# One output product for the last FFN of a four-FFN trunk: all its middle values at once, transposed by DMA, with P7 ahead of P3

## Chip, cores and metric

The kernel runs on one core of one Trainium2 chip. The metric is the device time of one execution in microseconds (us). All inputs lie in HBM at the start, and the output has to lie there at the end. A profiled execution also gives a span, from the first to the last instruction of the program, and a record of every instruction and DMA.

## What is computed

The reference is a trunk of two layers over 512 positions of width 1024, in float32. Each layer is a half-weighted SwiGLU FFN, a token mixer, and a second FFN; a final RMSNorm follows.

```python
def swiglu(x, w_in, w_out):
    g, u = jnp.split(x @ w_in, 2, axis=-1)       # w_in 1024 x 5632, w_out 2816 x 1024
    return (jax.nn.silu(g) * u) @ w_out

for i in range(DEPTH):                            # DEPTH = 2
    h = h + 0.5 * swiglu(rms_norm(h, ffn1_norm[i]), ffn1_w_in[i], ffn1_w_out[i])
    hn = rms_norm(h, mix_norm[i])
    m = recurrent_mixer(hn, ...) if i == 0 else spatial_gating_mixer(hn, ...)
    h = h + m
    h = h + 0.5 * swiglu(rms_norm(h, ffn2_norm[i]), ffn2_w_in[i], ffn2_w_out[i])
return rms_norm(h, final_norm)
```

So there are four FFNs, and the change is about the last of them and the final norm.

## The kernel before

**Number format.** Every float32 operand of a large product is split into a high part (`hi`, float32r, by ScalarE, line 99) and the rest (`lo`, by VectorE, line 90). A product is then three matmuls: hi x hi, lo x hi, hi x lo (lines 416 to 418). In the profile `whi`, `wlo` are the parts of a weight block, `hi`, `lo` those of a left operand.

**Seven products.** A product is cut into quarters and done with seven block products instead of eight (Strassen's method in Winograd's form): P1, P2, P5, P6, P3, P7, Q4 (function `seven`). Each has a left factor (A11, A12, S1, S2, S4, S3, A22, table `LEFT`) and a weight block; S1 = A21 - A22, S2 = S1 - A11, S4 = A12 + S2, S3 = -S2 - A22. Sums of weight blocks are made by loading one block and adding another, with an accumulating DMA of GpSimd (POOL, line 141) or on VectorE (`raw<-raw,raw`). The results gather in PSUM banks A (P1, then P6 and P7 on top), B (P2), C (P5, then P3 on top) and Q (Q4; in an output product with the final norm Q4 uses A). After a product, VectorE adds the bank to the hidden state `x`, which stays in SBUF.

**Sub-steps.** All work of TensorE is one list, `subs`: one entry is one product over one cut of the inner dimension, with 12 matmuls of 512 columns (6 where the cut has one block). At each entry the main loop at the end of the file emits, in this order, what is hooked as "pre", the splits of weight blocks up to three entries ahead (`SPLIT_AHEAD`), what is hooked as "mid" and "rest", new loads, the matmuls, and what is hooked as "end" and "late". Loads go out on SP in the order of the list, as long as fewer than ten blocks (`RAW_BUFS`) are held. Each engine works through its instructions in this order.

**An FFN.** The 22 blocks of 128 middle values are one pair (2 blocks, `pair_plain`, products named `p`) and five chunks of four (`chunk`, 14 sub-steps each). A chunk's result must be transposed before it can be the left operand of the output product (`out_blocks`). There are two ways. On TensorE, a 128x128 block at a time, through PSUM (`Group.turn`, line 270, tiles `e<-ident,c`) with a copy out by ScalarE. Or by the DMA crossbar (`Group.cross`): ScalarE sorts the halves of each float32 into two 16-bit planes (`pl`), SP issues a transposing DMA (`dt<-pl`), ScalarE merges the planes again five and six sub-steps later.

The first three FFNs collect all six groups of middle values and then do one output product over all of them (`FF_WHOLE`); all their transposes go by the crossbar, and the order of the 42 sub-steps is written out in `CHAIN`. The name `P62` is product P6 over cut 2; cut 0 is the pair and has half the work.

The fourth FFN is divided into three parts (`FF_PARTS`): pair and one chunk, two chunks, two chunks. Each part ends with its own output product of 14 sub-steps, in the order P1, P2, P6, P5, P7, Q4, P3 (`FinalNorm.ORDER`). In each part the first group goes by the crossbar, the second through TensorE.

**The end.** `FinalNorm` takes squares, roots and one Newton step as soon as rows of `x` are complete. P3 is the last product. Its first cut is held back (`held`), and in the last sub-step both cuts are multiplied for rows 0 and then for rows 1, with two matmuls by an identity (`gather`, line 1069) that add row block 1 of `x` into the bank. `last` then completes rows 0 and 1, and in between, for t = 0, it also scales and stores rows 2 and 3 (`both(2, 0)`, `scaled(3, 1)`, `both(3, 0)`).

Of the kernel before, what the change touches and what calls it, by code (L numbers as in the profile page):

```python
# [27 lines left out]

FF_PARTS = (("p", 4), (4, 4), (4, 4))
FF_WHOLE = (("p", 4, 4, 4, 4, 4),)

RAW_BUFS = 10
# [21 lines left out]
def trunk(ctx: ExitStack, tc: tile.TileContext, a: dict, out: bass.AP):  # L56
# [312 lines left out]
    def seven(block, cuts, left, w, posts, order=None, own=False, apart=False, joined=None, opening=None,  # L369
# [14 lines left out]
        def mm_of(prod, ci):  # L384
            name, fresh = banks[prod]
            pairs = cuts[ci]

            def mm(sub):
                if fresh and ci == 0:
                    for s in range(2):  # L390
                        bk[name, s] = bank(name)[:, :w]
                if prod == joined and ci == 0:
                    held.extend((sub, q, i) for q, i in enumerate(pairs))
                    return
                if opening and prod == "P1":
                    qs = list(enumerate(pairs))
                    for n, (q, i, m, s) in enumerate([(q, i, m, s) for q, i in qs for m in range(3) for s in range(2)]
                                                     if ci == 0 else
                                                     [(q, i, m, s) for m in range(3) for q, i in qs for s in range(2)]):
                        if n == (4 if ci else 6):  # L400
                            opening[ci]()
                        nc.tensor.matmul(bk[name, s], left(prod, i, s)[m == 1], (sub.lo if m == 2 else sub.hi)[:, q, :],
                                         start=(i, m) == (0, 0), stop=(i, m) == (cuts[-1][-1], 2))
                    for s in range(2 * ci):
                        posts[prod](s, bk[name, s])
                    return
                for s in range(2):
                    ps = bk[name, s]
                    k = {} if fresh else dict(skip_group_check=True)
                    if prod == joined and also is not None:  # L410
                        also(s, ps)
                    for sb, q, i in (held if prod == joined else []) + [(sub, q, i) for q, i in enumerate(pairs)]:
                        zh, zl = left(prod, i, s)
                        wh, wl = sb.hi[:, q, :], sb.lo[:, q, :]
                        end = i == cuts[-1][-1]
                        nc.tensor.matmul(ps, zh, wh, start=fresh and i == 0, stop=False, **k)  # L416
                        nc.tensor.matmul(ps, zl, wh, start=False, stop=False, **k)  # L417
                        nc.tensor.matmul(ps, zh, wl, start=False, stop=end, **k)  # L418
# [12 lines left out]
        for prod, ci in order:  # L431
# [3 lines left out]
            def new(k, n, plus=None, wait=2):  # L435
                b = lambda k, n: block(k, n, cuts[ci])
                return raw_of(b(k, n), [P, len(cuts[ci]), w], plus and b(*plus), wait)

            tile = then = tile_then = None
            if chain:  # L440
                if prod in ("P1", "P2"):
                    r = new(int(prod == "P2"), 0)
                elif prod == "P5":
                    r = raw[11, ci] = new(0, 0, (0, 1))
                elif prod == "P6":
                    r, tile, then = raw[11, ci], new(1, 1), block(1, 0, cuts[ci])
# [11 lines left out]
            elif prod == "P5":  # L458
# [10 lines left out]
            elif prod == "P6" and joined:  # L469

                tile, r, then = new(0, 1, (1, 1)), new(0, 0), block(1, 0, cuts[ci])
                raw[6, ci], raw[12, ci] = r, tile
            elif prod == "P6" and far(ci):
                r, then = raw[11, ci], block(1, 0, cuts[ci])
            elif prod == "P6":
                r, tile, then = raw[11, ci], new(1, 1), block(1, 0, cuts[ci])
                raw[22, ci] = tile
            elif prod == "P3":
                r = new(1, 1) if far(ci) or joined else raw[22, ci]
            elif prod == "P7":  # L480
                r = raw[12, ci] if joined or not own else new(0, 1, (1, 1), 2 + ci if far(ci) else 2)
            else:
                r = raw[6 if joined else 11, ci]
            subs.append(Sub(r, mm_of(prod, ci), None, tile, then, tile_then))
        return order

# [158 lines left out]
    def out_blocks(w, k0, groups, scale, norm=None, order=None, own=False, soon={}, swap=False, p2_lag=0, chain=False):  # L645
# [8 lines left out]
            bases[cut[0]] = r  # L654
            r += 2 * len(cut)

        gs, held, c5 = {}, [], []

        def block(k, c, cut):
            r0 = (bases[cut[0]] + k * len(cut)) * P  # L660
# [23 lines left out]
                take()  # L684

        def p5(s, ps):
            if ends:
                c5.append(ps)
            else:
                upd(2 + s, 1, ps, scale)  # L690

        def p6(s, ps):
            upd(s, 1, ps, -scale)
# [8 lines left out]
            final(s, 1, "A12", s)  # L702

        def p7(s, ps):
            if ends:
# [12 lines left out]

# [5 lines left out]
        def q4(s, ps):  # L724
            if held:
                second()
            upd(2 + s, 0, ps, scale)
            final(2 + s, 0, "A21", s)

        at0, ends = len(subs), hasattr(norm, "last")  # L730
        if ends:
            order = norm.ORDER
        order = seven(block, cuts, left_of(lambda: [gs[i] for i in range(len(n))]), 512,
                      dict(P1=p1, P2=p2, P5=p5, P6=p6, P3=p3, P7=p7, Q4=q4), order, own, not ends,
                      "P3" if ends else None, also=norm.gather if ends else None, chain=chain)

        sums_of = dict(P1=lambda ci: gs[ci].s2(), P2=lambda ci: gs[ci].s4(), P5=lambda ci: gs[ci].s3()) if chain else {}
# [195 lines left out]

    def ffn(w_in, w_out, norm):
        f0 = 0
        chain = not hasattr(norm, "last")
        all_parts = FF_WHOLE if chain else FF_PARTS
        for i, sizes in enumerate(all_parts):
            groups, p0, pair, first = [], f0, None, not subs
            for j, n in enumerate(sizes):  # L940
                if n == "p":
                    groups.append(Group(1))
                    groups[-1].whole = chain
                    pair = lambda g=groups[-1], f0=f0: pair_plain(w_in, f0, g, first)
                    if not first:
                        pair()
                    f0 += 2
                else:
                    groups.append(Group(n // 2))
                    groups[-1].whole = chain  # L950
# [3 lines left out]
            last, mixed = i == len(all_parts) - 1, "p" in sizes and not chain  # L954
            if mixed:
                groups.reverse()
            soon = {("Q4", len(groups) - 1): 3} if last and isinstance(norm, TileNorm) else {}
            gs = out_blocks(w_out, p0, [g.n for g in groups], 0.5, norm if last else None, CHAIN if chain else None,
                            own=True, soon=soon, swap=mixed, p2_lag=6 * mixed, chain=chain)
            gs.update(enumerate(groups))  # L960


    class FinalNorm:

        ORDER = [(p, ci) for p in ("P1", "P2", "P6", "P5", "P7", "Q4", "P3") for ci in range(2)]

        def __init__(self):
            self.gain, self.q, self.m, self.s = {}, {}, {}, {}  # L970
# [95 lines left out]
        def gather(self, t, ps):  # L1066
            if t == 1:
                for v in self.x:
                    nc.tensor.matmul(ps, self.eye, v, start=False, stop=False, skip_group_check=True)
# [620 lines left out]
```

## Time and profile before

| | us |
|---|---|
| median of 3 runs | 1577.5 (1577.21 to 1577.53) |
| profiled execution | 1577.6 |
| span of the profiled execution | 1575.9 |
| TensorE matmuls busy | 1567.9 |
| VectorE busy | 1314.0 |
| ScalarE busy | 1154.5 |
| start of the fourth FFN's matmuls | 1244.74 |
| end of the last matmul | 1569.47 |

The granted TensorE clock was 0.999 over the whole span. PE is TensorE, PEld its weight loads, DVE VectorE, ACT ScalarE, POOL GpSimd, SP SyncE. In the views, `out<-in` names tiles; times in a stretch count from the start of the span. Matmuls are pipelined, so that the records of two neighbours overlap, and the distance of their starts is what one costs.

### The profile page before, as it was taken

What the parts mean: (1) busy time and instruction counts of PE and PEld (TensorE: products, weight loads), DVE (VectorE), ACT (ScalarE), POOL (GpSimd) and SP (SyncE); (2) the same over time, 40 slices, a digit from 0 to 9 for tenths busy, and PEclk for the clock granted to TensorE, in tenths of its full rate; (3) what the DMA queues carried; (4) which work ended last, traced back from release to release, by engine and by line L of the source; (5) the groups of instructions that cost most, each with busy time, mean ns of one, the idle gap of its engine ahead of it and who ended that gap; (6) DMA issues with size and microseconds to landing.
All of it is one profiled execution on the core that took longest, in us unless ns stands there. A gap on an engine that the chain in (4) does not pass through costs nothing.

```text
span 1575.9 us, 20490 instructions
## 1 busy us (share of the span) xinstructions
PE 1567.9 (99%) x7149; PEld 1297.7 (82%) x7149; DVE 1314.0 (83%) x1759; ACT 1154.5 (73%) x1696; POOL 222.6 (14%) x201
## 2 busy tenths in 40 slices
PE   9999999999999999999999999999999999999998
PEld 7888888898888888888888888888888888888886
DVE  6977779878998777789787777798878988889788
ACT  7887786658777777786677777866886775675676
POOL 2111112200001111112201111022211011121120
PEclk9999999999999999999999999999999999999999
DMA  9888799944485888799948887899887576796793
GB/s 324 182 199 192 179 233 250 225 130 108 103 204 99 195 199 195 190 224 238 224 103 192 191 195 184 228 230 246 211 199 182 145 154 187 188 232 157 183 216 80
DMA packets 244776, 299.22 MB, mean 190 GB/s; under 512 B 91984, under 2 KB 117696, under 8 KB 244672
## 3 DMA queue, kind: packets, MB, share of 16 engines
q1 hardware_dynamic: 195168, 204.77, 42.9%
q0 software_dynamic: 47712, 91.30, 34.4%
q10 hardware_dynamic: 1792, 1.84, 0.3%
q8 instruction: 56, 0.92, 0.2%
q14 instruction: 48, 0.39, 0.1%
HBM read 275.84 MB, written 2.10 MB: 176 GB/s over the span
## 4 chain that ended last, share of the span: by engine, by line
PE 99%; DMA 0%; SPq 0%; ACT 0%; DVE 0%; issue 0%; DVEq 0%
PE A L416 15%; PE A L417 15%; PE A L418 15%; PE C L418 8%; PE C L417 8%; PE C L416 8%; PE p L888 6%; PE B L417 4%; PE B L418 4%; PE B L416 4%; PE r L228 2%; PE r L229 2%; PE r L230 2%; PE e L270 2%; PE Q L418 1%; PE Q L416 1%
## 5 line engine op out<-in xcount | busy, mean ns | idle before, releaser
L90 DVE TENSOR_TENSOR wlo<-raw,whi 128x1024 fp32r<-128x1024 f32 (+1 forms) x537 | 638.3, 1191 | 203.6 <-ACT whi L99 201.2
L99 ACT ACTIVATE whi<-raw 128x1024 fp32r<-128x1024 f32 (+1 forms) x537 | 553.7, 1032 | 261.2 <-PE C L417 75.0
L416 PE MATMUL A<-whi,hi 128*128 128x512 f32 x1016 | 398.9, 393 | 0.0
L417 PE MATMUL A<-whi,lo 128*128 128x512 f32 x1016 | 395.7, 389 | 0.0
L418 PE MATMUL A<-wlo,hi 128*128 128x512 f32 x1016 | 395.7, 389 | 0.0
L416 PEld LDWEIGHTS A<-whi,hi 128*128 128x128 f32 x1016 | 190.7, 188 | 44.4 <-ACT c L99 5.7
L418 PEld LDWEIGHTS A<-wlo,hi 128*128 128x128 f32 x1016 | 190.7, 188 | 40.1 <-DVE wlo L90 0.4
L417 PEld LDWEIGHTS A<-whi,lo 128*128 128x128 f32 x1016 | 190.8, 188 | 38.9 <-DVE lo L90 0.3
L416 PE MATMUL C<-whi,hi 128*128 128x512 f32 x560 | 218.1, 390 | 0.0
L417 PE MATMUL C<-whi,lo 128*128 128x512 f32 x560 | 217.9, 389 | 0.0
L418 PE MATMUL C<-wlo,hi 128*128 128x512 f32 x560 | 217.9, 389 | 0.0
L141 POOL DMA_DIRECT2D raw<-in_ffn_w_in_dram x82 | 99.0, 1209 | 727.3 <-DVE raw L90 453.6
L141 POOL DMA_DIRECT2D raw<-in_ffn_w_out_dram x72 | 83.9, 1199 | 342.0 <-DVE wlo L90 129.8
L90 DVE TENSOR_TENSOR raw<-raw,raw 128x1024 f32<-128x1024 f32 (+1 forms) x108 | 129.6, 1200 | 0.9
L90 DVE TENSOR_TENSOR lo<-a,hi 128x512 fp32r<-128x512 f32 (+1 forms) x188 | 122.3, 658 | 1.3 <-ACT hi L99 1.2
L417 PEld LDWEIGHTS C<-whi,lo 128*128 128x128 f32 x560 | 105.1, 188 | 22.1 <-DVE lo L90 0.2
L416 PEld LDWEIGHTS C<-whi,hi 128*128 128x128 f32 x560 | 105.1, 188 | 21.8
L418 PEld LDWEIGHTS C<-wlo,hi 128*128 128x128 f32 x560 | 105.1, 188 | 21.7
L99 ACT ACTIVATE hi<-a 128x512 fp32r<-128x512 f32 (+1 forms) x188 | 110.8, 597 | 15.9 <-DVE a L90 14.2
L417 PE MATMUL B<-whi,lo 128*128 128x512 f32 x280 | 109.1, 389 | 0.0
L416 PE MATMUL B<-whi,hi 128*128 128x512 f32 x280 | 109.0, 389 | 0.0
L418 PE MATMUL B<-wlo,hi 128*128 128x512 f32 x280 | 109.0, 389 | 0.0
(184 smaller groups left out, 2068.4 us busy)
## 6 DMA issues: line engine op xcount, KB each, us to landing
raw<-in_ffn_w_in_dram SPq DMA_DIRECT2D x161, 512.0 KB, 4.7
raw<-in_ffn_w_out_dram SPq DMA_DIRECT2D x100, 512.0 KB, 5.6
raw<-in_ffn_w_in_dram POOLq DMA_DIRECT2D x82, 512.0 KB, 7.7
raw<-in_ffn_w_out_dram POOLq DMA_DIRECT2D x60, 512.0 KB, 7.9
raw<-in_sg_w_in_dram SPq DMA_DIRECT2D x20, 512.0 KB, 8.6
raw<-in_ffn_w_in_dram SPq DMA_DIRECT2D x34, 256.0 KB, 6.7
raw<-in_rec_w_in_dram SPq DMA_DIRECT2D x16, 512.0 KB, 4.9
raw<-in_sg_w_in_dram POOLq DMA_DIRECT2D x12, 512.0 KB, 8.7
```

Of the source, the lines that this page charges most:

```text
L90: nc.vector.tensor_tensor(out=o, in0=x, in1=y, op=op)
L99: nc.scalar.activation(out=o, in_=x, func=f, **k)
L141: nc.gpsimd.dma_start(out=self.v, in_=src, accum_op=ALU.add)
L228: nc.tensor.matmul(ps, wh, xh, start=start, stop=False)
L229: nc.tensor.matmul(ps, wh, xl, start=False, stop=False)
L230: nc.tensor.matmul(ps, wl, xh, start=False, stop=stop)
L270: nc.tensor.transpose(ps[:, o : o + P], src(q, s), ident)
L416: nc.tensor.matmul(ps, zh, wh, start=fresh and i == 0, stop=False, **k)
L417: nc.tensor.matmul(ps, zl, wh, start=False, stop=False, **k)
L418: nc.tensor.matmul(ps, zh, wl, start=False, stop=end, **k)
L888: nc.tensor.matmul(bank_of(half, s), z, (sub.lo if m == 2 else sub.hi)[:, q, :], start=left[2] == "2" and (h, q, m) == (0, 0, 0), stop=lef ...
```

## The change

The fourth FFN works like the other three: one output product over all six groups, all transposes by the crossbar. Its 42 sub-steps have an order of their own (`LAST`), in which all of P7 is done before P3's cuts 2 to 5, so that P3 ends the list. P3 and P7 load blocks of their own (elsewhere P7 goes on with P3's). Of the six cuts of P3 the last but one is held back, and the identity matmuls stand in the last. Q4 has a bank of its own. Rows 2 and 3 are completed by hooks: the update from P7 (`second`) one sub-step after P7's end, their norm (`piece`) three and the scaling and storing (`rest`) four after it; `last` no longer does these. The gains of the final norm are loaded and halved 16 sub-steps earlier.

```diff
-FF_PARTS = (("p", 4), (4, 4), (4, 4))
 FF_WHOLE = (("p", 4, 4, 4, 4, 4),)
...
+LAST = [(s[:2], int(s[2])) for s in "P10 P11 P12 P13 P14 P20 P50 P51 P21 P15 P22 P23 P24 P60 P52 P53 P61 P25 P62 P54 P63 Q40 Q41 P55 P64 Q42 P65 Q43 P30 Q44 P31 P70 P71 Q45 P72 P73 P74 P75 P32 P33 P34 P35".split()]
...
-                if prod == joined and ci == 0:
+                if prod == joined and ci == len(cuts) - 2:
                     held.extend((sub, q, i) for q, i in enumerate(pairs))
                     return
...
-                    if prod == joined and also is not None:
+                    if prod == joined and also is not None and ci == len(cuts) - 1:
                         also(s, ps)
...
+                elif joined and prod in ("P3", "P7"):
+                    r = new(1, 1) if prod == "P3" else new(0, 1, (1, 1))
...
         def p7(s, ps):
-            if ends:
-
-                upd(2 + s, 1, ps, -scale)
-                if s == 1:
-                    for t, p in enumerate(c5):
-                        upd(2 + t, 1, p, scale)
-                final(2 + s, 1, "A22", s)
-                return
             upd(2 + s, 1, ps, -scale)
             held.append(ps)
-            if s == 1 and not isinstance(norm, TileNorm):
+            if ends and s == 1:
+                hook(now[0] + 1, "mid", second)
+                hook(now[0] + 3, "mid", lambda: (norm.piece(2, 0), norm.piece(3, 0)))
+                hook(now[0] + 4, "mid", norm.rest)
+            elif s == 1 and not isinstance(norm, TileNorm):
                 second()
             final(2 + s, 1, "A22", s)
...
+        def rest(self):
+            self.both(2, 0)
+            self.scaled(3, 1)
+            self.both(3, 0)
+
         def last(self, t, ps, scale):
...
             if t == 0:
-                self.both(2, 0)
-                self.scaled(3, 1)
-                self.both(3, 0)
                 self.newton(0, 1, slice(0, 1))
...
-    hook(len(subs) - 24, "late", last.load)
-    hook(len(subs) - 16, "rest", last.halve)
+    hook(len(subs) - 40, "late", last.load)
+    hook(len(subs) - 32, "rest", last.halve)
```

`second` is not new: it adds bank A, once P7 is in it, to the first half of rows 2 and 3.

More of the change, by code (lines that the diff above doesn't have):

```diff
@@ L468, in seven @@
                 r = raw[11, ci]
-            elif prod == "P6" and joined:
-                tile, r, then = new(0, 1, (1, 1)), new(0, 0), block(1, 0, cuts[ci])
-                raw[6, ci], raw[12, ci] = r, tile
             elif prod == "P6" and far(ci):
@@ L478, in seven @@
             elif prod == "P3":
-                r = new(1, 1) if far(ci) or joined else raw[22, ci]
+                r = new(1, 1) if far(ci) else raw[22, ci]
             elif prod == "P7":
-                r = raw[12, ci] if joined or not own else new(0, 1, (1, 1), 2 + ci if far(ci) else 2)
+                r = raw[12, ci] if not own else new(0, 1, (1, 1), 2 + ci if far(ci) else 2)
             else:
-                r = raw[6 if joined else 11, ci]
+                r = raw[11, ci]
             subs.append(Sub(r, mm_of(prod, ci), None, tile, then, tile_then))
@@ L655, in out_blocks @@
             r += 2 * len(cut)
-        gs, held, c5 = {}, [], []
+        gs, held = {}, []
         def block(k, c, cut):
@@ L686, in p5 @@
         def p5(s, ps):
-            if ends:
-                c5.append(ps)
-            else:
-                upd(2 + s, 1, ps, scale)
+            upd(2 + s, 1, ps, scale)
         def p6(s, ps):
@@ L727, in q4 @@
             upd(2 + s, 0, ps, scale)
-            final(2 + s, 0, "A21", s)
+            if not ends:
+                final(2 + s, 0, "A21", s)
         at0, ends = len(subs), hasattr(norm, "last")
-        if ends:
-            order = norm.ORDER
         order = seven(block, cuts, left_of(lambda: [gs[i] for i in range(len(n))]), 512,
-                      dict(P1=p1, P2=p2, P5=p5, P6=p6, P3=p3, P7=p7, Q4=q4), order, own, not ends,
+                      dict(P1=p1, P2=p2, P5=p5, P6=p6, P3=p3, P7=p7, Q4=q4), order, own, True,
                       "P3" if ends else None, also=norm.gather if ends else None, chain=chain)
@@ L935, in ffn @@
         f0 = 0
-        chain = not hasattr(norm, "last")
-        all_parts = FF_WHOLE if chain else FF_PARTS
-        for i, sizes in enumerate(all_parts):
+        ends = hasattr(norm, "last")
+        for sizes in FF_WHOLE:
             groups, p0, pair, first = [], f0, None, not subs
@@ L942, in ffn @@
                     groups.append(Group(1))
-                    groups[-1].whole = chain
+                    groups[-1].whole = True
                     pair = lambda g=groups[-1], f0=f0: pair_plain(w_in, f0, g, first)
@@ L949, in ffn @@
                     groups.append(Group(n // 2))
-                    groups[-1].whole = chain
+                    groups[-1].whole = True
                     chunk(w_in, f0, n, groups[-1],
@@ L953, in ffn @@
                     f0 += n
[L954 to L959, printed above, removed]
+            soon = {("Q4", len(groups) - 1): 3} if isinstance(norm, TileNorm) else {}
+            gs = out_blocks(w_out, p0, [g.n for g in groups], 0.5, norm, LAST if ends else CHAIN, own=True, soon=soon,
+                            chain=True)
             gs.update(enumerate(groups))
     class FinalNorm:
-        ORDER = [(p, ci) for p in ("P1", "P2", "P6", "P5", "P7", "Q4", "P3") for ci in range(2)]
         def __init__(self):
```

1 line of the change is left out of this document (removed).

## The prediction

> **What bounds the kernel now.** I read the page first: busy times of the engines, then the chain that ended last.
>
> ```profile
> PE 1567.9 (99%) x7149; PEld 1297.7 (82%) x7149; DVE 1314.0 (83%) x1759; ACT 1154.5 (73%) x1696; POOL 222.6 (14%) x201
> ...
> PE 99%; DMA 0%; SPq 0%; ACT 0%; DVE 0%; issue 0%; DVEq 0%
> ```
>
> TensorE (PE) is busy throughout and owns the chain. Next a table of stretches, cut at the starts of stages: the fourth FFN as a whole, its opening pair, then for comparison the five chunks of the second FFN and the output products of the second and the third.
>
> ```profile
> core 0: us, PE busy (x) PEld busy (x) DVE busy (x) ACT busy (x) POOL busy (x), PEclk, DMA share, GB/s
> 1244.74:1569.47 324.73, 324.73 (x1459) 268.16 (x1457) 279.87 (x360) 221.07 (x320) 44.99 (x38) 1.00 0.71 169
> 1244.74:1267.51 22.77, 22.77 (x107) 18.94 (x106) 19.45 (x36) 19.01 (x38) 0.00 (x0) 1.00 0.22 67
> 494.40:685.83 191.43, 191.43 (x841) 157.27 (x840) 144.74 (x158) 147.13 (x196) 25.02 (x21) 1.00 0.83 191
> 685.83:793.15 107.32, 107.32 (x487) 89.11 (x486) 98.03 (x130) 75.94 (x115) 19.93 (x17) 1.00 0.94 230
> 1007.36:1114.68 107.32, 107.32 (x487) 89.11 (x486) 98.78 (x130) 75.45 (x115) 25.02 (x22) 1.00 0.97 239
> ```
>
> PE is busy for the whole of every stretch, at full clock. Five chunks hold 840 matmuls of 512 columns: 191.43 / 840 = 0.228 us each, so a sub-step of 12 takes 2.73 us. The two output products are equal to 0.01 us although their DMA shares differ (0.94 and 0.97): there the transfers are heavy and hidden. The second and third FFN already work in the way that the change gives the fourth, so they price it.
>
> **The change part by part.** *Transposes.* The changed program has 48 PE transposes fewer, and every other PE count is unchanged (24 matmuls move from bank A to bank Q). The 48 are these (by tile, in the fourth FFN). The second fence has the transposes, for the norm that follows, inside the third FFN's output stage (groups of that stretch); the third is from the chain in order of time (start, us of length).
>
> ```profile
> L270 PE MATMUL e<-ident,c x48: 270/272/273, 1297.4 to 1533.1; 128*128 128x128 f32 x48
> ```
>
> ```profile
> L270 PE MATMUL e<-ident,x 128*128 128x128 f32 x24 | 3.1, 272 | 0.0
> ```
>
> ```profile
> 1404.42 0.87 PE e L270 x8
> ...
> 1485.09 0.44 PE A L416
> 1485.53 0.23 PE A L417
> ...
> 1561.00 0.44 PE A L418
> 1561.44 0.24 PE A L416
> ...
> 1566.26 0.47 PE C L1069 x2
> ```
>
> Each is 272 ns long, but eight follow one another in 0.87 us: 0.109 us each on the path. 48 x 0.109 = 5.2 us go. Against that, where a chunk follows a chunk directly, the chain has a first matmul of 0.44 instead of 0.23 us (1485.09): 0.2 us for a bank that is not yet free. Now two chunks of this FFN follow a chunk, afterwards four: +0.4 us. The same sort of step at 1561.00 is PE waiting for Q41's split on VectorE, the first of these three, 1.2 us long:
>
> ```profile
> 1559.67 3.48 DVE L90 TENSOR_TENSOR wlo<-raw,whi 128x1024 fp32r<-128x1024 f32 x3
> ```
>
> Afterwards these three splits are those of P33 to P35, the first of them 2.7 us ahead of its turn, and this wait goes: -0.2 us. Bottom up: -5.2 + 0.4 - 0.2 = -5.0 us.
>
> Top down, from stretches: pair 22.77, chunks 191.43, output product 107.32 less 24 x 0.109 = 2.6, plus the two matmuls with the identity (0.47), together 319.4; the old stretch has 324.73, of which some 0.2 is the drain of its last matmul (the other stretches end where the next matmul starts). 319.4 + 0.2 - 324.7 = -5.1 us (what rounding leaves open is 0.1). I take **-5.1 us** for PE.
>
> *Work that the transposes leave behind.* ScalarE gets 24 plane copies and 12 merges more, and 9 copies out of PSUM fewer; VectorE loses 30 updates of x (groups of the fourth FFN's stretch):
>
> ```profile
> L99 ACT ACTIVATE pl<-c 128x512 uint16<-128x512 uint16 x16 | 9.0, 622 | 1.9 <-DVE c L96 1.5 <-DVE c L90 0.4
> L99 ACT ACTIVATE a<-dt 128x1024 uint16<-128x1024 uint16 x6 | 7.1, 1177 | 0.0
> L99 ACT ACTIVATE a<-e 128x512 f32<-128x512 f32 x9 | 5.2, 583 | 0.0
> L96 DVE SCALAR_TENSOR_TENSOR x<-A,x 128x512 f32<-128x512 f32 x24 | 15.4, 682 | 1.5 <-PE A L418 1.5
> ```
>
> ScalarE: 24 x 0.62 + 12 x 1.18 - 9 x 0.58 = +23.8 us, from 221 to 245 of 320 us; VectorE: -30 x 0.68 = -20.5 us. Neither is late in the second and third FFN, which carry the same load, so both count nothing; without that cover, each us that ScalarE is late for a split would be a us of PE.
>
> *Transfers.* SP issues 18 DMAs more: 12 transposes, and 6 loads (5 of 512 KB, 1 of 256 KB), since P7 comes before P3 and needs a block of its own instead of P3's with something added. POOL's accumulates stay as many. The page's issues, with the median to landing, and the crossbar transposes' row by tile:
>
> ```profile
> raw<-in_ffn_w_out_dram SPq DMA_DIRECT2D x100, 512.0 KB, 5.6
> ...
> raw<-in_ffn_w_out_dram POOLq DMA_DIRECT2D x60, 512.0 KB, 7.9
> ```
>
> ```profile
> DMA to landing us min/median/max: 2.3/2.8/8.7
> ```
>
> A half's crossing is four plane copies (2.5 us) and two DMAs of 2.8 us in a row behind each other, some 8 us; the code asks for its first result five sub-steps (13.6 us) after the planes. The margin is 5 us at the median and none at the maximum. I count nothing. The Trainium skill speaks against this part: "VectorE: DVE Perf Modes", section "Rules for kernel authors", would leave a 128x128 transpose on TensorE where a PSUM destination will do, and its section "The three transpose paths" gives 390 ns against 1309 ns for the crossbar. By these figures as path times the sum would be 48 x 0.92 = 44 us worse, an estimate from that page; the trace differs, since on PE the transposes cost 0.109 us of the bound engine, and the crossbar's time is beside it.
>
> What waits in the new order? I stepped through the program's order of loads, splits and accumulates for both. POOL adds the block for Q44 when P64 is split, behind the accumulates of P70 and P71; Q44 is split five sub-steps later (Q40 is a half one): 4.5 x 2.73 = 12.3 us. In the old order of the second and third FFN the tightest is Q43, four steps, 3.5 x 2.73 = 9.6 us, and there ScalarE did wait (waits of 1040 to 1070 us), PE did not:
>
> ```profile
> ACT whi L99 <- DMA raw<-in_ffn_w_out_dram: 3.2, 1, 3.2
> ```
>
> So the new order is looser at its tightest place, and a split has three sub-steps in hand. Nothing counted.
>
> *The tail.* Afterwards P3 stays last (its last two cuts together, 24 matmuls and the identity pair, as now), but on VectorE the two scalings of rows 2 and 3 stand **ahead** of the update of row 0 that the last norm needs, instead of behind it. VectorE, then ScalarE, now:
>
> ```profile
> 1566.27 0.16 DVE L96 SCALAR_TENSOR_TENSOR fs<-ti,fs 128x2 f32<-128x2 f32 x1
> 1566.35 0.68 DVE L96 SCALAR_TENSOR_TENSOR x<-C,x 128x512 f32<-128x512 f32 x1
> 1566.95 1.41 DVE L96 SCALAR_TENSOR_TENSOR x<-x,fs,fg 128x512 f32<-128x512 f32 x2
> ...
> 1568.79 0.16 DVE L96 SCALAR_TENSOR_TENSOR fs<-ti,fs 128x1 f32<-128x1 f32 x1
> 1568.98 0.49 DVE L93 TENSOR_SCALAR x<-x,fs 128x512 f32<-128x512 f32 x1
> 1569.38 0.75 DVE L96 SCALAR_TENSOR_TENSOR x<-x,fs,fg 128x512 f32<-128x512 f32 x1
> ...
> 1570.81 0.16 DVE L96 SCALAR_TENSOR_TENSOR fs<-ti,fs 128x1 f32<-128x1 f32 x1
> 1571.01 0.75 DVE L96 SCALAR_TENSOR_TENSOR x<-C,fs,fg 128x512 f32<-128x512 f32 x1
> ```
>
> ```profile
> 1567.84 0.29 ACT L99 ACTIVATE fs<-fq,fm 128x1 f32<-128x1 f32 x1
> ```
>
> PE ends at 1569.47, and the last result is 2.3 us later (1571.76). Put the 1.41 us ahead: the update would end at 1567.03 + 1.41, less some 0.4 us by which the norm of rows 2 and 3 starts earlier (their last sums are taken two sub-steps before the last product, not straight before it): 1568.0. Its square and root take 1.1 us (1567.03 to 1568.13): 1569.1; two small steps 0.4, the scaling 0.49, the other 0.75: 1570.8; then the last small steps 0.65 and 0.75: 1572.2. That is **+0.5 us**; bounds: 0, if the norm of rows 2 and 3 starts 1 us earlier, and +0.9 without the 0.4. The stores of rows 2 and 3 go out earlier too:
>
> ```profile
> 1567.22 4.90 SPq L1032 DMA_DIRECT2D out_dram<-x  x7
> ```
>
> Seven issues in 4.90 us, 0.7 us apart, keep pace with 256 KB stores (0.87 us each by the page's queue row below), so the last waits for little; I count nothing, and -0.3 us as the bound.
>
> Sum: -5.1 + 0.5 = -4.6 us. The profiled execution took 1577.6 us (span 1575.9), the median of the runs is 1577.5: 1577.5 - 4.6 = **1572.9 us**, a span of 1571.3.
>
> **The rivals.**
>
> *Slower: the transfers come too late at Q44.* From the turn of P62 to that of P30 (nine and a half sub-steps, 25.9 us) the new order issues 9.5 loads (P70 to P75, P32 to P35; a half block counts 0.5) and 7.5 accumulates (six of P7, for Q44 and Q45).
>
> ```profile
> q1 hardware_dynamic: 195168, 204.77, 42.9%
> q0 software_dynamic: 47712, 91.30, 34.4%
> ...
> L90 DVE TENSOR_TENSOR wlo<-raw,whi 128x1024 fp32r<-128x1024 f32 (+1 forms) x537 | 638.3, 1191 | 203.6 <-ACT whi L99 201.2
> L99 ACT ACTIVATE whi<-raw 128x1024 fp32r<-128x1024 f32 (+1 forms) x537 | 553.7, 1032 | 261.2 <-PE C L417 75.0
> ```
>
> The shares are of 16 engines' span: 42.9% of 1575.9 us over 204.77 MB is 3.3 us per MB, 1.73 us per block of 0.52 MB; for accumulates 5.9 us per MB, 3.1 us. The burst is 16.4 + 23.3 = 39.7 us of transfer in 25.9: 13.8 us behind at its end. Q44's accumulate has 12.3 us, then 2.5 steps of reserve (6.8) less its two splitting operations (1.03 + 1.19), 16.9 in all, against a landing of 7.9: PE waits for what exceeds 9.0 us. That is 4.8 us, and the gain is gone (1577.7); if POOL also stands for one load's landing (5.6) in front of P71's accumulate, 10.4 us, 1583.3. Middle: **1580.5 us**. It decides from 13.6 us of backlog. For it: the DMA share of 0.97. Against: ten buffers throttle the loads, nothing follows this FFN, and the two output stages at 0.94 and 0.97 lost nothing. The Trainium skill, "DMA: Bandwidth & Descriptors", section "Issuing engines are not separate DMA queues", says that transfers of all issuing engines run on the same 16 DMA engines; by that rule the two queues' times add as above, and the two shares of 0.94 and 0.97 beside a calm PE are no safety. Chance 0.07; that part of the backlog shows (0.5 to 4 us of PE, 1573.5 to 1577): 0.12.
>
> *The tail costs nothing*, its lower bound: 1572.4. For it: rows 2 and 3 are complete two sub-steps earlier. Against: the three VectorE splits of P33 to P35 stand ahead of them. Chance 0.10.
>
> *The crossings are late*, at 8.7 us or over: six extra halves by 1 us beyond ScalarE's reserve, 1579. The ten crossings of the second and third FFN show no trace of it. Chance 0.02. That the change leaves the transposes on PE is excluded by the program's counts.
>
> **How the numbers follow.** The forecast has 0.69 and lies within 1572.2 to 1573.6. About 0.2% (3.2 us) is what a measurement of this kernel can tell from no change, so faster means below 1574.3: forecast, the free tail and a small part of the partial backlog, 0.80. Within 0.2%: the rest of that and the break-even end of the slower rival, 0.14. Slower: 0.06. The range reaches from 1571.7 (free tail, a little less waiting) to 1576.0, most of the partial backlog.
>
> **What would show it.** In the new profile: no transposes of c on PE after 1245 us; the stretch from the pair to the last matmul 319.6 us, out of which the output product 105.2; four steps of 0.44 at chunk starts; from PE's end to the last result 2.8 us instead of 2.3. PE idle or steps of 0.4 us and more inside the output product, ScalarE's splits waiting for DMA at Q44 or P7, would show the slower rival. A stretch over 321 us proves the sum wrong; a tail of 2.3 us proves only the tail wrong.

## The result, and the profile after

The changed kernel took 1572.31 us (median of six runs, 1571.74 to 1573.18) against 1577.57 us before on the same chips (1577.21 to 1578.9): a ratio of 0.9966, 95% interval 0.9953 to 0.9979, 5.3 us less. The forecast was 1572.9. The profiled execution took 1572.61 us with a span of 1570.9, 5.0 us under that of before, at the same granted clock, 0.999.

The page of the kernel after, its busy times and its chain:

```profile
PE 1563.1 (100%) x7101; PEld 1292.8 (82%) x7101; DVE 1296.7 (83%) x1732; ACT 1173.1 (75%) x1723; POOL 223.0 (14%) x201
...
PE 96%; issue 1%; DMA 1%; DVE 1%; POOL 0%; ACT 0%; POOLq 0%; ACTq 0%
```

TensorE has 48 matmuls fewer and 4.8 us less to do; ScalarE has 18.6 us more, VectorE 17.3 us less, and TensorE still owns the chain. (The 4% that TensorE lacks in it lie before 290.4 us: there it waited for a split, and the chain goes back through other engines from that point.) The table of stretches, cut as before: the fourth FFN as a whole, its pair, its five chunks, its one output product.

```profile
core 0: us, PE busy (x) PEld busy (x) DVE busy (x) ACT busy (x) POOL busy (x), PEclk, DMA share, GB/s
1245.01:1564.59 319.58, 319.58 (x1411) 263.16 (x1409) 262.40 (x332) 239.43 (x347) 44.98 (x38) 1.00 0.80 191
1245.01:1267.78 22.77, 22.77 (x107) 18.94 (x106) 19.48 (x36) 19.06 (x38) 0.00 (x0) 1.00 0.27 78
1267.78:1459.22 191.44, 191.44 (x842) 157.29 (x840) 144.78 (x158) 147.19 (x196) 26.22 (x22) 1.00 0.82 188
1459.22:1564.59 105.37, 105.37 (x465) 86.93 (x463) 98.14 (x140) 73.18 (x113) 18.76 (x16) 1.00 0.87 222
```

The stretch is 319.58 us instead of 324.73, so 5.15 us went inside the fourth FFN, with TensorE busy in all of it. Its first matmul stood 0.27 us later than before (1245.01 against 1244.74), from earlier stages that the change leaves alone: the wait at 290 us costs some 0.5 us, and the kernel before has none there. From the last matmul (1564.59) to the last result (1566.88), here called the tail, it is 2.29 us, as before, and from the last matmul to the end of the span 6.32 instead of 6.43. 0.27 - 5.15 - 0.11 = -5.0 us, the whole difference of the spans.

The tile of the transposes, in the fourth FFN, has only those of the norm in front of it:

```profile
L270 PE MATMUL e<-ident,x x16: 270/272/273, 1244.2 to 1251.3; 128*128 128x128 f32 x16
```

The chain has the four long first matmuls at the chunks' ends, and a fifth, shorter, at the last chunk's (start, length, line):

```profile
1300.58 0.44 PE A L416
...
1338.90 0.44 PE A L416
...
1377.21 0.44 PE A L416
...
1415.52 0.44 PE A L416
...
1453.84 0.32 PE A L416
```

Each of these matmuls is the first of Q4, two sub-steps before the chunk's end.

VectorE at the end: the root of rows 2 and 3, their scalings, the update of row 0, and then the last norm.

```profile
1560.40 0.16 DVE L96 SCALAR_TENSOR_TENSOR fs<-ti,fs 128x2 f32<-128x2 f32 x1
1560.60 1.42 DVE L96 SCALAR_TENSOR_TENSOR x<-x,fs,fg 128x512 f32<-128x512 f32 x2
1561.93 0.69 DVE L96 SCALAR_TENSOR_TENSOR x<-C,x 128x512 f32<-128x512 f32 x1
...
1565.68 0.22 DVE L96 SCALAR_TENSOR_TENSOR ti<-fs,ti 128x1 f32<-128x1 f32 x1 [0.17 <-ACT fs L99]
...
1566.13 0.75 DVE L96 SCALAR_TENSOR_TENSOR x<-C,fs,fg 128x512 f32<-128x512 f32 x1
```

The norm of rows 2 and 3 was done 4.03 us before TensorE's end (1560.56 against 1564.59); before the change 3.04 us (1566.43 against 1569.47). The two scalings stand ahead of the update, as foreseen, but the norm ahead of them was done a full microsecond earlier than before, not 0.4 us. The update starts 2.66 us before TensorE's end instead of 3.12, 0.46 us later, and the last small step still waits for ScalarE's root (0.17 us), not for VectorE.

ScalarE's splits of weight blocks in the output product, where the slower rival was expected; the bracket is its idle time and what ended it:

```profile
1527.75 2.01 ACT L99 ACTIVATE whi<-raw 128x1024 fp32r<-128x1024 f32 x2 [4.31 <-DMA raw<-in_ffn_w_out_dram]
...
1535.76 1.06 ACT L99 ACTIVATE whi<-raw 128x1024 fp32r<-128x1024 f32 x1 [1.64 <-DMA raw<-in_ffn_w_out_dram]
...
1543.76 1.06 ACT L99 ACTIVATE whi<-raw 128x1024 fp32r<-128x1024 f32 x1 [0.32 <-DMA raw<-in_ffn_w_out_dram]
...
1547.82 1.06 ACT L99 ACTIVATE whi<-raw 128x1024 fp32r<-128x1024 f32 x1 [1.96 <-DMA raw<-in_ffn_w_out_dram]
```

They are those of Q44 (with P31's), Q45, P74 and P75. For Q44's block ScalarE waited 4.31 us. VectorE's part of that split, and Q44's first matmul:

```profile
1528.84 1.23 DVE L90 TENSOR_TENSOR wlo<-raw,whi 128x1024 fp32r<-128x1024 f32 x1 [2.19 <-ACT whi L99]
```

```profile
1529.94 0.39 PE L416 MATMUL Q<-whi,hi 128*128 128x512 f32 x1
```

The split ended at 1530.07, 0.13 us after that matmul had begun (the matmul that needs the low part is the third, at 1530.39). TensorE lost nothing, but of the cover, which the prediction counted at three sub-steps (8.2 us; 2.5 of them, 6.8 us, at Q44), only tenths were left. How far this place moves from run to run, the second experiment shows.

### The profile page after: what moved, and what is told of

Its sections match the earlier page's. It is cut to its first block, busy times and chain, and to the rows that moved or that the text cites. A ratio compares the mean times of both kernels' runs of the same rounds, so it can differ in the third digit from the quotient of the medians.

```text
span 1570.9 us, 20410 instructions
## 1 busy us (share of the span) xinstructions
PE 1563.1 (100%) x7101; PEld 1292.8 (82%) x7101; DVE 1296.7 (83%) x1732; ACT 1173.1 (75%) x1723; POOL 223.0 (14%) x201
## 4 chain that ended last, share of the span: by engine, by line
PE 96%; issue 1%; DMA 1%; DVE 1%; POOL 0%; ACT 0%; POOLq 0%; ACTq 0%
PE A L416 14%; PE A L417 14%; PE A L418 14%; PE C L417 8%; PE C L418 8%; PE C L416 8%; PE p L878 6%; PE B L417 4%; PE B L418 4%; PE B L416 4%; PE r L228 2%; PE r L229 2%; PE r L230 2%; PE e L270 1%; PE Q L418 1%; PE Q L417 1%
```

## The experiments

Two theories stood at the start. A: the gain is the transposes' own time on TensorE, and the scalings and splits that moved lie in idle time. B: the order of the list and its transfers cost or bring something too, and the two cancel. "After" is the changed kernel; every edit is made to it, except the last two, which are made to the version ahead of them.

**The transposes back on TensorE.** Each half of chunks 1, 3 and 5 is transposed on TensorE too, into a tile that nothing reads.

```diff
+            if getattr(g, "extra", False):
+                def turns(hs=list(hs)):
+                    for k in range(2):
+                        g.turn(lambda q, s: hs[s][:, (k * g.n + q) * P : (k * g.n + q + 1) * P])
+                hook(n, "end", turns)
...
+                    groups[-1].extra = ends and j in (1, 3, 5)
```

> The changed kernel with 48 extra TensorE transposes of 128x128 in the fourth FFN, eight each after the first and second half of the first, third and fifth chunk, into a PSUM bank that nothing reads; the crossbar still does the work. Theory A (the gain is TensorE time of 48 transposes at 0.109 us in a queue that has no slack): the stretch from the fourth FFN's first to its last matmul grows from 319.6 to 324.8 us, the time from 1572.3 to 1577.5. Rival B (the gain came from elsewhere, such as fewer updates of x on VectorE, and the transposes slip into waits): under 1 us longer.

Measured: 1579.22 us (1578.22 to 1580.64), before 1577.77: 1.0008, interval 0.9998 to 1.0017. All of the gain is gone again. The stretch of the fourth FFN is 7.09 us longer than after. TensorE before the output product:

```profile
1464.21 0.39 PE L418 MATMUL A<-wlo,hi 128*128 128x512 f32 x1
1465.99 1.23 PE L270 MATMUL e<-ident,c 128*128 128x128 f32 x8 [1.39 <-DVE c L90]
1466.97 0.48 PE L416 MATMUL A<-whi,hi 128*128 128x512 f32 x1
```

The six groups of eight cost about 0.88 us each, 5.3 together, as theory A has it. The rest is a wait of its own: the last chunk's transposes stand in TensorE's queue behind a difference that VectorE has yet to make. From 1464.21 to 1466.97 it is 2.76 us where 0.23 + 0.87 would do, 1.7 us lost. The kernel before has no such wait: in its fourth FFN TensorE never waits for a `c` of VectorE. So the 1.7 us belong to the place where this edit puts the transposes, and the 5.3 us are what they cost by themselves. The Trainium skill, "VectorE: DVE Perf Modes", section "Rules for kernel authors", would leave these transposes on TensorE; this run does not agree with it here, where TensorE sets the end.

**The scalings at their old place**, behind the update of row 0.

```diff
-                hook(now[0] + 4, "mid", norm.rest)
...
             if t == 0:
+                self.rest()
```

> The changed kernel with the scaling and storing of rows 2 and 3 put back into the last step, behind the update of row 0 on VectorE as in the kernel before. Theory A (rows 2 and 3 are normalised 1 us earlier than before, so that the moved work just fits ahead of the update): from the last matmul's end to the last result 2.3 us, as now, within 0.1. Rival B (the moved work lies on the path, as the prediction had it): 0.5 us shorter, 1.8 us.

Measured (one run): 1572.38 us, tail 2.29, stretch 319.58: nothing changes. VectorE now waits at the update:

```profile
1561.18 0.69 DVE L96 SCALAR_TENSOR_TENSOR x<-C,x 128x512 f32<-128x512 f32 x1 [0.85 <-PE C L418]
```

The update starts 3.17 us before TensorE's end, half a microsecond earlier than after, and nothing comes of it. The moved work is off the path on both sides.

This run shows one thing more. Up to P75 its program is that of after, and yet Q44's block came in time:

```profile
1525.42 2.01 ACT L99 ACTIVATE whi<-raw 128x1024 fp32r<-128x1024 f32 x2 [2.21 <-DMA raw<-in_ffn_w_out_dram]
```

ScalarE's split begins 66.4 us into the output product instead of 68.5, and the split is complete 1.96 us ahead of Q44's turn. In three other profiles with the same list and transfers (the transposes back, more VectorE work, and the first edit of the plane copies, below) it is 0.80, 0.24 and 0.50 us behind. So the lateness at Q44 moves by over 2 us between runs of one order; no run shows why.

**How much VectorE could still take there:** two more additions of 128x512 (1.28 us) ahead of `second`.

```diff
+                hook(now[0] + 1, "mid", lambda: [tt(slot(name="junk"), xt(0, 0), xt(0, 0), ALU.add) for _ in range(2)])
                 hook(now[0] + 1, "mid", second)
```

> The changed kernel with two extra VectorE additions of 128x512 (1.28 us together, result unused) ahead of the last update of rows 2 and 3. Theory A (VectorE has a reserve of only about 0.2 us in the chain from rows 2 and 3 to the last result): from the last matmul's end to the last result 3.3 to 3.4 us instead of 2.3. Rival B (VectorE has more than 1.3 us in hand there): 2.3 us still.

Measured (one run): 1572.92 us, tail 3.41.

```profile
1561.03 1.41 DVE L96 SCALAR_TENSOR_TENSOR x<-x,fs,fg 128x512 f32<-128x512 f32 x2
1562.36 0.68 DVE L96 SCALAR_TENSOR_TENSOR x<-C,x 128x512 f32<-128x512 f32 x1
...
1566.38 0.75 DVE L96 SCALAR_TENSOR_TENSOR x<-C,fs,fg 128x512 f32<-128x512 f32 x1
```

TensorE ends at 1563.72, the last result comes at 1567.13. Of 1.28 us, 1.12 show: the reserve was 0.16 us, the same as the 0.17 that VectorE waited for ScalarE. The chain that the prediction drew through the tail is the right one, and the update could be some 0.6 us later than before (0.46 + 0.16) at no cost; the prediction's own working left it 0.5. (The time of the run moved by less, since its fourth FFN began 0.9 us earlier than in the profile after, at 1244.09.)

**Q44 one entry earlier in the list,** to see whether its block really comes at the last moment.

```diff
-LAST = "... Q43 P30 Q44 P31 ..."
+LAST = "... Q43 Q44 P30 P31 ..."
```

> The changed kernel with Q44 one entry earlier in the order, ahead of P30 (1.36 us). Theory A (the DMA that adds the block for Q44 is the tightest transfer, its split is complete only 0.13 us after Q44's first matmul begins, so no reserve is left): TensorE waits 1.2 to 1.6 us at Q44 and the stretch of the output product grows from 105.4 to about 106.8 us. Rival B (ten buffers and three splits ahead take it up): no wait, 105.4 us.

Measured (one run): 1572.02 us, output product 105.56, only 0.18 us of waiting at Q44. The waits of 1510 to 1560 us:

```profile
ACT whi L99 <- DMA raw<-in_ffn_w_out_dram: 6.7, 4, 3.5
```

Mostly a miss for theory A: the block came earlier as well. ScalarE's split of it begins 67.5 us into the output product, 1.0 us earlier than after, which makes up most of the 1.36. Whether the place in the list did that is not shown, since this moment moves by 2 us without any edit (66.4 us with the scalings at their old place).

**P7 without its additions:** what makes the block late? P7's second block is not added.

```diff
-                    r = new(1, 1) if prod == "P3" else new(0, 1, (1, 1))
+                    r = new(1, 1) if prod == "P3" else new(0, 1)
```

> The changed kernel without the six accumulating DMAs for P7 in the last output product (P7 multiplies with the loaded block alone, the second block is left out of its weights). Theory A (Q44's block comes late because P7's loads and accumulates stand ahead of its own on POOL and on the DMA engines): ScalarE's 4.3 us wait for a DMA ahead of Q44's split is gone or under 1 us, and the split is complete at least 3 us ahead of its turn; the time stays within 0.3 us of 1572.3, since TensorE did not wait there. Rival B (the DMA engines are simply saturated by loads): the wait stays over 3 us.

Measured (one run): 1572.57 us, output product 105.38. The longest waits of 1510 to 1560 us:

```profile
POOL raw L141 <- DVE wlo L90: 14.1, 2, 9.7
ACT whi L99 <- PE A L417: 6.9, 5, 1.7
```

No split waits for a DMA any more, and Q44's is 2.15 us ahead of its turn instead of 0.13 behind. (Theory A had expected 3 us; VectorE, which works there without a gap, does not come to it earlier.) One run alone would not show that P7's accumulates make it late, since a run with them had 1.96 us in hand. But the two versions at the end, which have none of P7's accumulates ahead of Q44's, are 2.1 us ahead too: three profiles of three, against one of the six that have them in this order. The time does not move, since nothing had been lost to it.

**P7's blocks loaded twice,** the second time into a tile that nothing reads: how much more transfer is there room for?

```diff
+            if getattr(self, "twice", False):
+                for q in range(k):
+                    nc.sync.dma_start(out=slot(name="junk"), in_=self.src[:, q, :])
...
+                    r.twice = prod == "P7"
```

> The changed kernel with P7's six weight blocks of the last output product loaded a second time from SP, into slots that nothing reads (11 loads of 256 KB, 2.9 MB, some 9.5 us of transfer at 3.3 us per MB). Theory A (around Q44 the transfers run behind, and TensorE has no reserve left there): TensorE waits 3 to 9 us in the output product, at Q44 and P70 to P75, and the stretch of 105.4 us grows to 108 to 114. Rival B (the lateness at Q44 is POOL's order, not transfer time): under 1 us of waiting.

Measured (one run): 1576.73 us, the output product 4.6 us longer (109.98). The waits of 1510 to 1562 us (three lines added ahead: L419 is the first matmul, L421 the third):

```profile
ACT whi L99 <- DMA raw<-in_ffn_w_out_dram: 14.3, 5, 6.1
...
PEld A L419 <- ACT whi L99: 2.2, 1, 2.2
...
PEld Q L419 <- ACT whi L99: 1.0, 1, 1.0
PEld A L421 <- DVE wlo L90: 1.0, 1, 1.0
```

5.5 more blocks, by the prediction's 1.73 us some 9.5 us of transfer, cost 4.6 us of TensorE, 1.7 at Q44 (bank Q) and 2.9 at P75 (bank A). The 1.7 at Q44 is little more than the 1.3 that a version below loses there without any load added, so what the added loads cost shows surely only at P75. The slower rival is a real mechanism, at Q44 and in P7; the change stopped just short of it.

**The long first matmul at the chunks' ends.** The profile after showed what makes these 0.44 us. ScalarE and TensorE at the end of the second chunk:

```profile
1335.68 1.67 ACT L99 ACTIVATE pl<-c 128x512 uint16<-128x512 uint16 x3 [0.76 <-DVE c L96]
...
1337.26 1.04 ACT L99 ACTIVATE whi<-raw 128x1024 fp32r<-128x1024 f32 x1
...
1338.21 0.57 ACT L99 ACTIVATE c<-A 128x512 f32<-128x512 f32 x1
...
1338.83 0.19 PEld L416 LDWEIGHTS A<-whi,hi 128*128 128x128 f32 x1 [0.36 <-ACT c L99]
1338.83 0.50 PE L416 MATMUL A<-whi,hi 128*128 128x512 f32 x1
```

The copy that empties bank A stands in ScalarE's queue behind a weight split and, ahead of that, plane copies for the crossing of the half that is just complete, and Q4's first matmul waits for that bank. The edit queues these plane copies one entry later, for every chunk of all four FFNs but the very first:

```diff
-            g.cross(half, hs, (n, "mid"), ((n + 5, "mid"), (n + 6, "mid")), ())
+            g.cross(half, hs, (n + 1, "late") if late else (n, "mid"), ((n + 5, "mid"), (n + 6, "mid")), ())
...
-                left_blocks(group, ht, 0, 3 if opening else 1, whole=whole)
+                left_blocks(group, ht, 0, 3 if opening else 1, whole=whole, late=not opening)
```

> The changed kernel with the plane copies of the first half of each chunk's result (all four FFNs, but the very first chunk) moved behind ScalarE's copies of P7 out of bank A, in ScalarE's order. Theory A (the two matmul steps of 0.33 instead of 0.23 us at Q4's start, where a chunk follows a chunk, are TensorE waiting until ScalarE has copied P7 out of bank A, and this copy waits behind a weight split that in turn waits behind four plane copies): some 0.2 us at each of about 15 chunk ends go, -2 to -3 us, 1569.8 us. Rival B (the wait is of another kind, or what is moved makes the merges or the next splits late): no gain, or up to 2 us slower.

Measured: 1574.84 us (1574.52 to 1578.01), before 1577.74: 0.9986, interval 0.9977 to 0.9995, so 2.5 us more than after. What TensorE's weight loads wait for, in the whole span, after and then here:

```profile
PEld A L416 <- ACT c L99: 6.6, 19, 0.4
```

```profile
PEld A L417 <- DVE lo L90: 7.5, 6, 1.8
```

The 19 waits for the copy are gone, and others have come, four of them long: at P13 of each of the four output products the transposed halves of the last chunk, whose crossing now starts later, aren't split yet (in the fourth FFN TensorE stands 1.6 us). So the last chunk of each FFN keeps its old place in the next edit:

```diff
+                          ..., late=j < 5 and not (first and j == 1)
```

> As e6, but the last chunk of each FFN, which the output product follows, keeps the old place of its plane copies. Theory A (e6 removed the waits at Q4 and lost 1.6 us at P13 of every output product, because the last chunk's copies then stood ahead of P13's split): the 0.2 us go at 15 chunk ends, no wait at P13, -3 us against the changed kernel: 1569.3 us; the fourth FFN's stretch 318.8 instead of 319.6 us. Rival B (the moved copies make merges late in the chunk that follows): a part of it comes back, 1570.5 to 1572.5.

Measured: **1568.35 us** (1568.24 to 1570.9), before 1577.64: 0.9944, interval 0.9931 to 0.9958. It beats both kernels, after by 4.0 us; its slowest run (1570.9) is below the fastest of after (1571.74). Its waits of weight loads:

```profile
PEld Q L418 <- DVE wlo L90: 1.0, 1, 1.0
...
PEld A L416 <- ACT c L99: 1.0, 4, 0.2
...
PEld Q L416 <- ACT whi L99: 0.6, 1, 0.6
PEld A L418 <- DVE wlo L90: 0.5, 1, 0.5
```

6.6 us of waiting for the copy became 1.0, and up to the output product of the fourth FFN the kernel is 4.2 us shorter (from the first matmul of the first pair, 1436.1 us instead of 1440.3). The profiled run itself took 1570.06 us: in its output product TensorE waited 1.3 us for Q44 and 0.4 us for P75, and the product took 107.07 us. What was 0.13 us late at Q44 after, at no cost, is a loss here. Three of the five runs lie within 0.11 us (1568.24 to 1568.35); whether the other two (1570.06 and 1570.9) are those that waited, the one profile can't say.

**Those waits taken away, twice,** both times in the version just measured (the last chunk of each of the four FFNs keeps its place). First, P7's accumulates go to POOL two entries later, behind that of Q44:

```diff
-                    r = new(1, 1) if prod == "P3" else new(0, 1, (1, 1))
+                    r = new(1, 1) if prod == "P3" else new(0, 1, (1, 1), 4)
```

> As e7, with P7's accumulating DMAs queued two entries later, so that on POOL those for Q44 and Q45 stand ahead of those of P70 and of P71 on. Theory A (Q44 is late because its accumulate stands behind P70's and P71's on POOL and on the DMA engines, and this lateness is the difference of up to 2.6 us between runs of e7): Q44's split complete at least 2 us ahead of its turn, no wait of TensorE in the output product over 0.2 us, median 1568.2 us or less, and runs within 1 us of each other. Rival B (the transfers as a whole run behind): the wait moves to P7's splits, and the runs spread as before.

Measured: 1569.96 us (1569.33 to 1571.06), before 1577.7: 0.9953, interval 0.9939 to 0.9966. Q44's split is 2.1 us ahead, but TensorE loses 0.3 us in P74 and 1.3 in P75, and the product takes 106.94 us. The longest of these waits is that of P75's third matmul:

```profile
1548.07 0.50 PE L418 MATMUL A<-wlo,hi 128*128 128x512 f32 x1 [0.53 <-DVE wlo L90]
```

ScalarE's splits of P72 to P75:

```profile
1533.92 1.06 ACT L99 ACTIVATE whi<-raw 128x1024 fp32r<-128x1024 f32 x1 [3.63 <-DMA raw<-in_ffn_w_out_dram]
...
1537.69 1.06 ACT L99 ACTIVATE whi<-raw 128x1024 fp32r<-128x1024 f32 x1 [2.19 <-DMA raw<-in_ffn_w_out_dram]
...
1541.67 1.06 ACT L99 ACTIVATE whi<-raw 128x1024 fp32r<-128x1024 f32 x1 [0.37 <-DMA raw<-in_ffn_w_out_dram]
...
1545.69 1.06 ACT L99 ACTIVATE whi<-raw 128x1024 fp32r<-128x1024 f32 x1 [1.92 <-DMA raw<-in_ffn_w_out_dram]
```

They come every 3.8 to 4.0 us, each as its accumulate lands, where a sub-step is 2.73 us. In these two profiles the order on POOL only chooses which sub-step pays (1.7 us there, 1.6 here), as rival B has it. Second, P7 takes the block that P3 loads anyway and adds it on VectorE, so that P7 has no accumulates:

```diff
-                    r = new(1, 1) if prod == "P3" else new(0, 1, (1, 1))
+                    if (33, ci) not in raw:
+                        raw[33, ci] = new(1, 1)
+                    r, tile = (raw[33, ci], None) if prod == "P3" else (new(0, 1), raw[33, ci])
```

> Planes late as in the fastest version so far (all chunks but the last of the fourth FFN), and P7's second block is the one that P3 has loaded anyway, added on VectorE; P7 takes no accumulating DMA any more. That leaves out five and a half accumulates, which land 4.0 us apart (22 us of POOL's queue), and adds 5.5 additions of 1.2 us on VectorE (6.6 us, 98 of the 105 us of the output product then busy). Theory A, the accumulates were what came late: no PE wait over 0.2 us at Q44 and P70 to P75, output product 105.4 us, median 1568.2 or less and runs within 1 us of each other. Theory B, VectorE becomes the late engine: P7's or P3's matmuls wait for its splits, output product 106 to 108 us, median 1569 to 1571.

Measured: 1568.85 us (1568.37 to 1570.21), before 1577.7: 0.9943, interval 0.9929 to 0.9956. The output product here and with P7's accumulates:

```profile
1456.41:1561.97 105.56, 105.56 (x465) 86.82 (x463) 103.69 (x146) 73.31 (x113) 11.77 (x10) 1.00 0.72 193
```

```profile
1455.01:1562.08 107.07, 106.27 (x465) 86.69 (x463) 97.82 (x140) 73.14 (x113) 18.79 (x16) 1.00 0.88 216
```

It is 1.5 us shorter, with the DMA share at 0.72 instead of 0.88; the one wait left is 0.18 us at P75, where VectorE, busy 103.69 of 105.56 us, is 0.43 us late. For the waits theory A is right. The median is not better, and the runs are spread over 1.8 us, not 1: the profiled run, the slowest of the five, had the first matmul of the first pair at 20.40 us instead of 18.92, 1.5 us lost before the first product. The two versions can't be told apart by their times; what makes the start vary stays open.

## Why the prediction was right, and where it was not

- **TensorE, -5.1 us: right.** The stretch measured 319.58 (foretold 319.6), the output product 105.37 (105.2, and 0.2 for the drain of its last matmul), -5.15 us. The transposes put back cost 5.3 us by themselves, against 5.2 for the term. The four steps of 0.44 are there, and the bank is their cause, but they stand at Q4, near the chunks' ends, not at chunk starts; the fifth, 0.32, was not foretold and is 0.1 us. Pricing the new fourth FFN by the second and third, which already worked in its way, gave nearly the exact number. (The two times that the prediction took from the Trainium skill, "VectorE: DVE Perf Modes", section "The three transpose paths", are given there for bf16; the blocks here are float32.)
- **The tail, +0.5 us: wrong, 0.0 measured.** The chain was right: the experiment with more VectorE work shows that the tail follows it, with 0.16 us to spare. The step that failed is its input, "some 0.4 us by which the norm of rows 2 and 3 starts earlier": it was 1.0 us. The prediction had named 1 us as the point where the term is 0, and gave that case 0.10. The 0.4 was a guess about where two hooks fall between VectorE's splits of P33 to P35; it might have been worked out from the queue by the same stepping as the transfers.
- **ScalarE and the crossings: nothing, as counted,** though mis-sized: ScalarE has 18.4 us more in the stretch, not 23.8, among other things because records in a row overlap (three plane copies above take 1.67 us, not 1.86). VectorE has 17.5 less, not 20.5: beside the overlap, six half-width differences (`c<-c` of 128x256, 10 instead of 4) came, and three additions after transposes went. The chunks take 191.44 us as in the second FFN. But an average of 75% says little of a queue: the place of the plane copies in it is worth 4 us over the whole kernel.
- **Transfers at Q44: no loss, as forecast, but "looser at its tightest place" was wrong.** ScalarE waited 4.31 us there, against 3.2 at the tightest place of before, and almost nothing was left. The stepping through the list compared where an accumulate is issued with where it is needed, and left out how long it would take; from 1500 us on the median to landing was 10.7 us, where the page of before has 7.9. The burst of the slower rival was there. That rival's place holds, and nearly its prices (below). TensorE's loss was 0.0, not 4.8: of the 9.5 loads and 7.5 accumulates that it counted in 25.9 us, 6.5 and 5.5 were issued in them, and accumulates were still landing at 1547.8, one sub-step before their turn. That the forecast of no loss came true here was in part luck: the reason given for it was wrong, and a few tenths were left. Doubled loads and the version with the chunk ends mended turned the same place into 1.7 and 1.3 us of waiting.
- **The stores of rows 2 and 3:** -0.1 us by the rest of the span, within the bounds of 0 and -0.3.

The median came out 0.6 us below the forecast: the tail's 0.5 and the stores' 0.1. (The 0.27 us of the earlier stages stands in the difference of the two profiles, 5.0 us, and not in that of the medians, 5.3.)

## What to carry to other kernels

Work that only the bound engine does is priced by the distance of its starts, and a stage that already works in the new way is the best price list. Where a change moves work off the bound engine, look in the queues of the others for what the bound engine is waiting for behind it: here an in-order ScalarE queue held a bank for 0.2 us some nineteen times, and one entry's delay of work that nobody needed yet was worth almost as much as the change itself. And before such a delay, find the one place where its result is needed soon.

## What the runs showed of the hardware

Accumulates that run beside plain loads land later, though a block takes no more of the engines' time. The DMA queues of the kernel after from 1532 to 1547.7 us (packets, MB, share of 16 engines):

```profile
q0 software_dynamic: 944, 1.80, 62.0%
q1 hardware_dynamic: 1272, 2.45, 45.6%
```

The accumulates (q0) took 62.0% of 15.7 us for 1.80 MB, 2.8 us for a block of 0.52 MB, and the loads 1.5 us for one; the prediction had 3.1 and 1.73. In the same stretch of the kernel before, accumulates were alone: 45.0% for 1.21 MB, 3.1 us for a block, and they landed 5.8 us after their issue. Beside loads they landed 10.6 us after it, and 4.0 us apart. "DMA: Bandwidth & Descriptors" of the Trainium skill, section "Issuing engines are not separate DMA queues", says that the queues share the engines; the trace agrees: the shares of the two add up to more than the whole (62.0% + 45.6%), and loads doubled on SP made an accumulate of POOL late (2.9 us lost at P75). Beside that, a stage whose DMA share was 0.87 on the mean had 32 us in it at 1.04 (1515.6 to 1547.7), and it was there that the splits came late.
